# Two transformer blocks in one launch: TensorE's instructions keep the task list's order

## The chip, the cores and the metric

The kernel runs on one core of a Trainium2 chip. A core has a matrix engine (TensorE, PE in the profile), three engines for everything else (VectorE or DVE, ScalarE or ACT, GpSimd or POOL) and DMA queues that are fed by SyncE (SP). Each engine works through its own list of instructions in order, and the engines wait for each other by semaphores. The metric is the device time of one execution in microseconds.

## The reference

A sequence of 256 tokens of width 1024 goes through two blocks, all in float32. The first has two layers; the second mixes a linear recurrence with attention and ends in a gated MLP. Cut to what matters here:

```python
# first block, layer l (pooling mixer for l = 0, local attention for l = 1)
proj = rmsnorm(h, norm_mix[l]) @ w_in[l]
main, mq = proj[..., :768], proj[..., 768:]
main_out = pool_mixer(main, pool_w[l], pool_scale[l])        # l = 0: window sums, then 4 groups of 192 x 192
main_out = swa_sink_attention(q, k_shared, v_shared, sinks)  # l = 1: 12 heads of 64, window 128
mem_out = memory_attention(rmsnorm(mq), mk, mv)              # 4 heads of 64, 256 memory positions
h = h + concat([main_out, mem_out]) @ w_out[l]
h = h + relu(rmsnorm(h) @ w_up[l]) ** 2 @ w_down[l]          # width 4096

# second block
hq, hf, hi, hg, aq, ak, av, gl = split(rmsnorm(x) @ w_in)    # 8 heads of 128 each, gates of 2 x 1024
y_hg = hgrn2_mix(hq, hf, hi, hg, ...) @ w_branch_hg          # recurrence; its output times silu(hg)
y_at = moba_attention(rmsnorm(aq), rmsnorm(ak), av, rel) @ w_branch_attn   # one block of 256: causal
x = x + (sigmoid(gl[0]) * y_hg + sigmoid(gl[1]) * y_at) @ w_out
x = x + (silu(h2 @ w_gate) * (h2 @ w_up)) @ w_down           # h2 = rmsnorm(x)
```

## The kernel before

**Products.** A large product x @ w is split into rounded high and low parts and summed as xh·wh + xl·wh + xh·wl (L152, `mm`), in a rounded float32 type. Weights come by DMA into `raw` tiles; ScalarE casts the high half `wh` (L245), VectorE subtracts for the low half `wl` (L246). The activations get `xh` and `xl` in the same way. Scores, attention values, the pooling product and transposes (L159, `tr`) stay in plain float32; in the trace such a matmul has two records.

**Banks.** TensorE writes only to PSUM, of which there are eight banks of 512 float32 columns per partition: four with the tag `acc` and four with the tag `mm`, taken in turn. Instructions that share a bank are ordered by the framework: a matmul that writes into a bank which VectorE or ScalarE has yet to read, as the program has it, waits for that read, also where other columns of the bank are meant.

**What sets the order.** The parts of the work (a projection, one half of the tokens in an attention, an MLP) are Python generators, added to a list by `line.add(rank, task)`. `line.run` asks, at each step, the task of lowest rank whose time has come for its next piece. Time is `line.now`, which only `mm` and `tr` advance (by columns at the full clock); a task gives its own guess of how long its results take by `yield 6.0` and the like. This is the task list's order. After it, the framework's scheduler orders the instructions of each engine anew, by its own model of when each could start. Only in the start, inside `with tc.manual_schedule(engines={ET.DVE, ET.Activation, ET.Pool, ET.PE})` (L727), does it leave all four engines in the order written.

**The places that the change touches.**

- `pool_mix` (layer 0). For three banks in turn, two column pieces k each: the products with `pw` and `u` (L152), then ScalarE takes the high half out of the bank (L941, `xh<-mm,cols`) and VectorE the low half (L942, `xl<-mm,cols,xh`). The even and the odd piece of a bank are of one bank. Some pieces consist of two products of 128 rows, others of four of 64 rows.
- `mem_attention`. Two halves of the tokens (tt), four heads: four score products into two `acc` banks, alternating between them (and between the upper and lower 64 rows), maxima (L884), exponentials (L889), reciprocals (L891), scaling, transposes, values.
- `swa` (layer 1). `score(i)` gives two heads a bank each; VectorE reads each with bias and minimum in one instruction (L1036).
- `attend` (second block). `score(hp)` puts two heads into one bank, one behind the other. For each, VectorE adds the position bias, takes the minimum and writes to SBUF (L1411, with the accumulator's read as a second instruction), ScalarE exponentiates (L1413):

```python
for i in range(2):
    mm(ps[:, i, :nk], aq[tt][:, hd, :], ak[hd // 4][:, hd % 4, :nk])
    V.tensor_tensor_reduce(sc[:, i, :nk], ps[:, i, :nk], rel..., nm[:, c])
    A.activation(sc[:, i, :nk], sc[:, i, :nk], AF.Exp, ..., accum_out=sm[:, c])
V.reciprocal(sm[:, c2], sm[:, c2])
```

- `sides` runs beside `attend` in the list: weight products of the recurrence's gate, whose sigmoid (L1480) needs another function table on ScalarE than the exponential, and the two multiplications L1481 and L1482 on VectorE.

Of the kernel before, what the change touches and what calls it, by code (L numbers as in the profile page):

```python
# [41 lines left out]
def kernel(  # L42
# [8 lines left out]
    nc = tc.nc  # L51
    V, A, G, PE = nc.vector, nc.scalar, nc.gpsimd, nc.tensor

    const = ctx.enter_context(tc.tile_pool(name="const", bufs=1))
    wpool = ctx.enter_context(tc.tile_pool(name="wpool", bufs=1))
    keep = ctx.enter_context(tc.tile_pool(name="keep", bufs=1))
# [94 lines left out]
    def mm(out_, lhsT, rhs, start=True, stop=True):  # L151
        PE.matmul(out_, lhsT, rhs, start=start, stop=stop)  # L152
        n = math.prod(rhs.shape[1:])
        m = math.prod(lhsT.shape[1:])
        side_by_side = 4 if m <= 32 else 2 if m <= 64 else 1
        line.now += max(n, min(m, 64)) / 2400.0 * (1 if rhs.dtype == F32R else 4) / side_by_side + 0.0025
# [5 lines left out]
    def acc_bank():  # L162
        return psum.tile([P, 512], F32, tag="acc", name="acc", bufs=4)

    def mm_bank():
        return psum.tile([P, 512], F32, tag="mm", name="mm", bufs=4)
# [7 lines left out]
    def tok(tt):  # L174
        return slice(tt * P, (tt + 1) * P)
# [51 lines left out]
    def load_units(segs, nk, row0, g, apart=0):  # L227
        for k0 in range(0, nk, KU):
            raw = wpool.tile([P, KU, 512], F32, tag="raw", name="raw", bufs=5)
            c = 0  # L230
            for w, c0, cw in segs:
                r = w[row0 + k0 * P: row0 + (k0 + KU) * P, c0:c0 + cw].rearrange("(k p) c -> p k c", p=P)
                for k in range(KU if k0 < apart else 1):
                    ks = slice(k, k + 1) if k0 < apart else slice(0, KU)
                    nc.sync.dma_start(raw[:, ks, c:c + cw], r[:, ks, :])  # L235
                c += cw
            wh = wpool.tile([P, KU, 512], F32R, tag="wh", name="wh", bufs=8)
            wl = wpool.tile([P, KU, 512], F32R, tag="wl", name="wl", bufs=8)

            tc.cur_priority += 30  # L240
            if g is None:
                n = 1 if k0 < apart else KU
                for k in range(0, KU, n):
                    ks = slice(k, k + n)
                    A.copy(wh[:, ks, :], raw[:, ks, :])  # L245
                    V.tensor_sub(wl[:, ks, :], raw[:, ks, :], wh[:, ks, :].bitcast(F32))  # L246
            else:
                for k in range(KU):
                    gk = gcols[:, g + k0 + k:g + k0 + k + 1]
                    A.activation(wh[:, k, :], raw[:, k, :], AF.Copy, scale=gk)  # L250
                    V.scalar_tensor_tensor(wl[:, k, :], raw[:, k, :], gk, wh[:, k, :].bitcast(F32),  # L251
                                           op0=ALU.mult, op1=ALU.subtract)
            tc.cur_priority -= 30
            yield [(wh[:, k, :], wl[:, k, :]) for k in range(KU)]
# [61 lines left out]
    def lin(acc, xt, w, start=True, stop=True):  # L316

        n = len(w)
        for k in range(n):
            (xh, xl), (wh, wl) = xt[k], w[k]  # L320
            mm(acc, xh, wh, start and k == 0, False)
            mm(acc, xh, wl, False, False)
            mm(acc, xl, wh, False, stop and k == n - 1)
            if k % 2:
                yield 0
# [29 lines left out]
    def ktiles(t, tt=None):  # L355
        ts = slice(0, S) if tt is None else tok(tt)
        return [(t[0][:, k, ts], t[1][:, k, ts]) for k in range(t[0].shape[1])]
# [347 lines left out]
    def raw_T():  # L705

        return [act.tile([P, KT // 2, S], F32, tag="raw_T", name="raw_T", bufs=4) for _ in range(2)]

    def load_T(t, src, k, n):
        nc.sync.dma_start(t[k // 4][:, k % 4:k % 4 + n, :],  # L710
                          src[k * P:(k + n) * P, :].rearrange("(k p) t -> p k t", p=P))
# [11 lines left out]
        V.tensor_sub(xs[1][:, o, :], r, xs[0][:, o, :].bitcast(F32))  # L723

    pw = act.tile([P, 6, 192], F32, tag="pw", name="pw")
    ET = mybir.EngineType
    with tc.manual_schedule(engines={ET.DVE, ET.Activation, ET.Pool, ET.PE}):  # L727

        x_raw, m_raw = raw_T(), raw_T()

        warm = mm_bank()
        for _ in range(12):
            PE.matmul(warm[:, :P], ones, ones, start=True, stop=True)

        def units_of(i, **a):
            key, w = plan[i][:2]
            ready[key] = []
            units = load_units(*w, **a)

            def more():  # L740
                ready[key] += next(units)
                return ready[key][-KU:], len(ready[key]) - KU

            return more

        def columns_T(ps, xs, w, k, c0):

            for i, (wh, wl) in enumerate(w):
                xh, xl = ktiles(xs)[k + i]
                c = slice(c0, c0 + P)  # L750
                for j, (a, b) in enumerate(((wh, xh), (wh, xl), (wl, xh))):
                    mm(ps, a[:, c], b, k + i + j == 0, k + i == KT - 1 and j == 2)

        def rows(accs, xs, w, k):
            for tt in range(TT):
                run(lin(accs[tt], ktiles(xs, tt)[k:k + KU], w, k == 0, k + KU == KT))

        load_T(x_raw, xT, 0, 2)
        ups = [acc_bank()[:, :S] for _ in range(4)]
        more = units_of(0, apart=1)  # L760
        for k in range(0, KT, KU):
            if k:
                load_T(x_raw, xT, k, 2)
            split_raw(x_raw, xs0, k, 2, G_MIX)
            w, _ = more()
            for i in range(4):
                columns_T(ups[i], xs0, w, k, i * P)
        ups += [mm_bank()[:, :S] for _ in range(2)]
        more = units_of(1)
        pool_short()  # L770
        ws = []
        for k in range(0, KT, KU):
            w, _ = more()
            ws += w
            for i in range(2):
                columns_T(ups[4 + i], xs0, w, k, i * P)
        for tt in range(TT):
            nc.sync.dma_start(h[tt], x[0, tok(tt), :])
        nc.sync.dma_start(cols, columns)
        for k in range(0, KT, 4):  # L780
            load_T(m_raw, memT, k, 4)

        dg = act.tile([P, TT, P], F32, tag="dg", name="dg")
        nx = [Norm(h[tt]) for tt in range(TT)]
        for tt in range(TT):
            for c in range(2):
                nx[tt].add(c)
            x_r[tt] = nx[tt].rstd()
            V.tensor_scalar(dg[:, tt, :], ident, x_r[tt], None, op0=ALU.mult)
        split_raw(m_raw, mem_set, 0, 4)  # L790
        qs = mm_bank().rearrange("p (t c) -> p t c", t=TT)
        rb = act.tile([P, S], F32, tag="rb", name="rb")
        more = units_of(2)

        def queries(tt):
            run(lin(qs[:, tt, :], ktiles(xs0, tt), [(wh[:, 256:], wl[:, 256:]) for wh, wl in ws]))

        queries(0)
        ps = mm_bank()[:, :S]
        for tt in range(TT):  # L800
            PE.matmul(ps[:, tok(tt)], ones, dg[:, tt, :], start=True, stop=True)
        A.copy(rb, ps)
        queries(1)
        for i in range(2):
            V.tensor_tensor(u[:, i, :], ups[i], rb, ALU.mult)
        w, k = more()
        accs1 = [acc_bank() for _ in range(2)]
        rows(accs1, mem_set, w, k)
        split_raw(m_raw, mem_set, 4, 4)
        for i in range(2, 4):  # L810
            V.tensor_tensor(u[:, i, :], ups[i], rb, ALU.mult)
        rows(accs1, mem_set, *more())
        for i in range(4, 6):
            V.tensor_tensor(u[:, i, :], ups[i], rb, ALU.mult)
        for tt in range(TT):
            A.activation(mq[tt], qs[:, tt, :], AF.Copy, scale=x_r[tt])
        m = [act.tile([P, D], F32, tag="raw_T", name="mem", bufs=4) for _ in range(TT)]
        tc.keep_in_program_order(nc.sync.dma_start(m[0], mem[0, tok(0), :]))
        rows(accs1, mem_set, *more())
        tc.keep_in_program_order(nc.sync.dma_start(m[1], mem[0, tok(1), :]))  # L820
        mem_r[0] = row_norm(m[0])
        rows(accs1, mem_set, *more())
        mem_r[1] = row_norm(m[1])
        nc.gpsimd.dma_start(pw, pool_w[0].rearrange("g a d -> (g a) d").rearrange("(j p) d -> p j d", p=P))
        for e in mem_there:
            e.at()
# [761 lines left out]
```

## Time and profile before

| | |
|---|---|
| median of 3 runs | 1039.11 us (1039.04 to 1039.41) |
| the profiled execution | 1038.09 us, of which 1036.1 us from its first to its last instruction (the span) |
| TensorE busy | 1025.5 us (99%) |
| VectorE, ScalarE, GpSimd busy | 639.7 (62%), 562.8 (54%), 99.1 us (10%) |
| DMA | 186.40 MB, 180 GB/s on average |
| mean granted TensorE clock | 0.999 of full speed |
| chain that ended last | TensorE 96%, VectorE 1%, GpSimd 1%, DMA 1% |

Busy time of TensorE includes time in which a matmul is in the array while the next could not yet start at its best, so 99% does not say that the array is at its peak. The chain that ended last goes back from the last instruction to what released it, step by step; 96% on TensorE means that nearly everywhere the next matmul waited only for the one ahead of it.

### The profile page before, as it was taken

The numbers are of one execution on the slowest core, as the hardware profiler recorded it, in microseconds if no ns is written. First come the engines' busy times: TensorE is split into PE (matmuls) and PEld (weight loads), VectorE is DVE, ScalarE is ACT, GpSimd is POOL, SyncE is SP. The second block draws the span as 40 slices with busy tenths as digits, with TensorE's granted clock in tenths as the row PEclk, the third lists the DMA queues.
The fourth block names the chain that finished last, engine by engine and source line by source line (L and its number), as shares of the span: only waits on it lengthen the run. The fifth ranks groups of instructions, "written<-read, shape, count | busy, mean of one in ns | idle before, by whom it ended". The sixth has DMA issues, their size and how long they took to land.

```text
span 1036.1 us, 18404 instructions
## 1 busy us (share of the span) xinstructions
PE 1025.5 (99%) x7352; PEld 904.8 (87%) x7352; DVE 639.7 (62%) x1001; ACT 562.8 (54%) x901; POOL 99.1 (10%) x143
## 2 busy tenths in 40 slices
PE   8999999999999999999999999999999999999998
PEld 8768989998876788899988988888999988999997
DVE  5886655556668666464576569847635766464552
ACT  6775554454678654454465444758644555344351
POOL 1515000000143000000000004330000000000000
PEclk9999999999999999999999999999999999999999
DMA  9754556546642258656557544344365566565741
GB/s 320 269 181 136 181 184 211 191 163 204 202 164 82 57 189 317 210 185 213 173 182 235 193 165 153 119 137 145 119 203 180 169 196 210 164 211 164 234 144 41
DMA packets 107749, 186.40 MB, mean 180 GB/s; under 512 B 6792, under 2 KB 31632, under 8 KB 107664
## 3 DMA queue, kind: packets, MB, share of 16 engines
q1 hardware_dynamic: 106560, 180.43, 53.4%
q0 software_dynamic: 1104, 4.80, 1.4%
q8 instruction: 57, 0.93, 0.4%
q14 instruction: 28, 0.23, 0.1%
HBM read 182.58 MB, written 2.63 MB: 179 GB/s over the span
## 4 chain that ended last, share of the span: by engine, by line
PE 96%; DVE 1%; POOL 1%; DMA 1%; ACT 0%; issue 0%; SPq 0%; ACTq 0%
PE acc L152 59%; PE mm L152 33%; PE mm L159 3%; DMA raw<-in_w_in_dram 1%; POOL win L921 0%; DVE wl L251 0%; DVE wl L246 0%; POOL st L419 0%; POOL win L920 0%; POOL st L348 0%; ACT wh L250 0%; DVE win L921 0%; ACT wh L245 0%; ACT xh L722 0%; SPq L235 0%
## 5 line engine op out<-in xcount | busy, mean ns | idle before, releaser
L246 DVE TENSOR_TENSOR wl<-raw,wh 128x1024 fp32r<-128x1024 f32 (+1 forms) x315 | 378.1, 1223 | 172.2 <-ACT wh L245 165.6
L245 ACT CAST wh<-raw 128x1024 fp32r<-128x1024 f32 (+1 forms) x315 | 322.3, 1047 | 170.7 <-PE acc L152 101.8
L152 PE MATMUL mm<-xh,wh 128*128 128x256 f32 x752 | 208.4, 277 | 0.0
L152 PE MATMUL mm<-xl,wh 128*128 128x256 f32 x752 | 208.0, 277 | 0.0
L152 PE MATMUL mm<-xh,wl 128*128 128x256 f32 x752 | 207.9, 277 | 0.0
L152 PEld LDWEIGHTS mm<-xh,wh 128*128 128x128 f32 x752 | 141.2, 188 | 1.4 <-issue 0.4
L152 PEld LDWEIGHTS mm<-xl,wh 128*128 128x128 f32 x752 | 141.3, 188 | 1.0
L152 PEld LDWEIGHTS mm<-xh,wl 128*128 128x128 f32 x752 | 141.3, 188 | 0.0
L152 PE MATMUL acc<-wh,xh 128*128 128x512 f32 x336 | 138.3, 412 | 1.2 <-ACT wh L250 1.2
L152 PE MATMUL acc<-wh,yl 128*128 128x512 f32 x342 | 134.8, 394 | 0.0
L152 PE MATMUL acc<-wl,yh 128*128 128x512 f32 x342 | 134.0, 392 | 0.0
L152 PE MATMUL acc<-wl,xh 128*128 128x512 f32 x336 | 132.4, 394 | 1.1 <-DVE wl L251 1.1
L152 PE MATMUL acc<-wh,yh 128*128 128x512 f32 x342 | 133.4, 390 | 0.0
L152 PE MATMUL acc<-wh,xl 128*128 128x512 f32 x336 | 132.6, 395 | 0.0
L152 PE MATMUL acc<-xh,wh 128*128 128x256 f32 x416 | 117.1, 281 | 1.0 <-ACT wh L245 1.0
L152 PE MATMUL acc<-xh,wl 128*128 128x256 f32 x416 | 116.5, 280 | 1.2 <-DVE wl L246 1.2
L152 PE MATMUL acc<-xl,wh 128*128 128x256 f32 x416 | 116.2, 279 | 0.0
L152 PEld LDWEIGHTS acc<-xh,wl 128*128 128x128 f32 x416 | 78.7, 189 | 1.8 <-DVE wl L246 1.8
L152 PEld LDWEIGHTS acc<-xh,wh 128*128 128x128 f32 x416 | 78.6, 189 | 1.6 <-ACT wh L245 1.6
L152 PEld LDWEIGHTS acc<-xl,wh 128*128 128x128 f32 x416 | 78.2, 188 | 0.0
L152 PEld LDWEIGHTS acc<-wh,xh 128*128 128x128 f32 x336 | 63.2, 188 | 16.0 <-issue 2.5
L152 PEld LDWEIGHTS acc<-wl,yh 128*128 128x128 f32 x342 | 64.2, 188 | 13.7
(240 smaller groups left out, 1277.6 us busy)
## 6 DMA issues: line engine op xcount, KB each, us to landing
raw<-in_w_in_dram SPq DMA_DIRECT2D x87, 512.0 KB, 4.7
raw<-in_w_up_dram SPq DMA_DIRECT2D x64, 512.0 KB, 4.8
raw<-in_w_down_dram SPq DMA_DIRECT2D x64, 512.0 KB, 4.8
raw<-in_w_out_dram SPq DMA_DIRECT2D x24, 512.0 KB, 4.6
raw<-in_w_ffn_gate_dram SPq DMA_DIRECT2D x44, 256.0 KB, 4.3
raw<-in_w_ffn_up_dram SPq DMA_DIRECT2D x44, 256.0 KB, 4.6
raw<-in_w_ffn_down_dram SPq DMA_DIRECT2D x22, 512.0 KB, 5.3
raw<-in_w_mem_kv_dram SPq DMA_DIRECT2D x8, 512.0 KB, 9.4
```

The source lines that it names most:

```text
L152: PE.matmul(out_, lhsT, rhs, start=start, stop=stop)
L159: PE.transpose(out_, in_, ident)
L245: A.copy(wh[:, ks, :], raw[:, ks, :])
L246: V.tensor_sub(wl[:, ks, :], raw[:, ks, :], wh[:, ks, :].bitcast(F32))
```

## The change

The whole kernel is put under `manual_schedule` for TensorE, and TensorE leaves the inner one:

```diff
+    ET = mybir.EngineType
+
+    ctx.enter_context(tc.manual_schedule(engines={ET.PE}))
     const = ctx.enter_context(tc.tile_pool(name="const", bufs=1))
...
     pw = act.tile([P, 6, 192], F32, tag="pw", name="pw")
-    ET = mybir.EngineType
-    with tc.manual_schedule(engines={ET.DVE, ET.Activation, ET.Pool, ET.PE}):
+    with tc.manual_schedule(engines={ET.DVE, ET.Activation, ET.Pool}):
```

TensorE's instructions then stand in the order in which the task list gives them. The scheduler still orders the other engines outside the start. Line numbers after the change are higher by 3 up to L723 and by 2 from there on (L152 is then L155, L942 is L944, L1411 is L1413), numbers in the names by 2. On the DMA queue SP nothing moves; VectorE and ScalarE change little. TensorE's order differs in three places.

First place, TensorE in the layer-0 mixer. `mm_733` is the first bank of the pooling product (`mm_735` after the change), `mm_768` and `mm_777` the second and third (`mm_770`, `mm_779`); `acc_718` is a weight product, `acc_746` and `acc_747` are memory scores. Before:

```order
L152 MATMUL mm_733<-u_94,pw_98 128x256 [waits DMASW0_49,PE_49]
L152 MATMUL mm_733<-u_94,pw_98 128x256
L152 MATMUL mm_768<-u_94,pw_98 128x256 [waits DVE_49,Activation_49]
L152 MATMUL mm_768<-u_94,pw_98 128x256 [waits DVE_49]
L152 MATMUL acc_718<-wh_546,xh_88 128x512
L152 MATMUL mm_777<-u_94,pw_98 64x256 [waits DVE_49,Activation_49]
L152 MATMUL acc_746<-mkT0_568,mqT_593 128x256 [waits Activation_49]
```

The same place after the change:

```order
L155 MATMUL mm_735<-u_96,pw_100 128x256 [waits DMASW0_49,PE_49]
L155 MATMUL mm_735<-u_96,pw_100 128x256
L155 MATMUL mm_735<-u_96,pw_100 64x256 [waits DVE_49]
L155 MATMUL mm_735<-u_96,pw_100 64x256 x3
L155 MATMUL acc_748<-mkT0_570,mqT_595 128x256 [waits Activation_49]
L155 MATMUL acc_749<-mkT0_570,mqT_595 128x256
L155 MATMUL acc_748<-mkT0_570,mqT_595 128x256
L155 MATMUL acc_749<-mkT0_570,mqT_595 128x256
L155 MATMUL mm_770<-u_96,pw_100 128x256 [waits PE_49]
L155 MATMUL mm_770<-u_96,pw_100 128x256
L155 MATMUL mm_770<-u_96,pw_100 128x256 [waits DVE_49]
```

The second piece of the first bank (64x256) stands directly behind the first piece; before, it comes eighteen rows later. The wait on DVE is for the low half (L944) of the first piece.

Second place, TensorE in the local attention of layer 1: `acc_3229` and `acc_3233` are the scores of two heads of one group (`acc_3231` and `acc_3235` after). Before, the second one stood behind six weight products and two transposes. After the change:

```order
L155 MATMUL acc_3231<-skT_2810,qT_3169 128x256 [waits DVE_49]
L155 MATMUL acc_3235<-skT_2810,qT_3169 128x256 [waits DVE_49]
L155 MATMUL acc_3138<-wh_2918,xh_1112 128x512
L155 MATMUL acc_3138<-wl_2919,xh_1112 128x512
L155 MATMUL acc_3138<-wh_2918,xl_1113 128x512
```

The second score now stands ahead of the weight products, with its own wait on VectorE.

Third place, TensorE in the attention of the second block: `acc_7481` is the bank of two heads of the first token half, `acc_7494` that of the second half (`acc_7483` and `acc_7496` after); `acc_7435` is the gate's weight product. Before:

```order
L152 MATMUL acc_7481<-ak_5528,aq_5526 128x128 [waits Activation_49]
L152 MATMUL acc_7494<-ak_5528,aq_5527 128x256 [waits Activation_49]
L152 MATMUL acc_7435<-wh_7380,xh_3770 128x512
L152 MATMUL acc_7481<-ak_5528,aq_5526 128x128 [waits DVE_49]
L152 MATMUL acc_7435<-wl_7381,xh_3770 128x512
L152 MATMUL acc_7494<-ak_5528,aq_5527 128x256 [waits DVE_49]
L152 MATMUL acc_7435<-wh_7380,xl_3771 128x512
```

The third head pair of each token half after the change (`acc_7551`, `acc_7569`; `mm_7545` and `mm_7561` are transposes of the first pair):

```order
L162 MATMUL mm_7545<-ident_76,sc_7482 128x128 x2
L155 MATMUL acc_7551<-ak_5531,aq_5528 128x128
L155 MATMUL acc_7551<-ak_5531,aq_5528 128x128 [waits DVE_49]
L162 MATMUL mm_7561<-ident_76,sc_7495 128x128 x4
L155 MATMUL acc_7569<-ak_5531,aq_5529 128x256
L155 MATMUL acc_7569<-ak_5531,aq_5529 128x256 [waits DVE_49]
```

In each of the eight pairs the two heads now stand directly one behind the other, and the second waits for VectorE's read of the first.

## Rows read from the trace of the kernel before

**Rows 1.** The page: span, and each engine's busy time, share and instructions

```profile
span 1036.1 us, 18404 instructions
...
PE 1025.5 (99%) x7352; PEld 904.8 (87%) x7352; DVE 639.7 (62%) x1001; ACT 562.8 (54%) x901; POOL 99.1 (10%) x143
```

**Rows 2.** Waits of TensorE, largest and last of seven: us in total, times, longest

```profile
PE acc L152 <- ACT wh L250: 1.2, 1, 1.2
...
PE mm L152 <- issue: 0.5, 1, 0.5
```

**Rows 3.** Timeline, TensorE, place 1: start us, us, engine, line, operation, idle before

```profile
53.43 1.86 PE L152 MATMUL mm<-u,pw 128*128 128x256 f32 x8
54.94 0.58 PE L152 MATMUL acc<-wh,xh 128*128 128x512 f32 x1
...
56.08 1.13 PE L152 MATMUL acc<-mkT,mqT 64*128 64x256 f32 x8
...
58.70 1.22 PE L152 MATMUL mm<-u,pw 64*64 64x256 f32 x4 [0.92 <-DVE u L926]
59.85 1.13 PE L152 MATMUL acc<-mkT,mqT 64*128 64x256 f32 x4
60.91 0.51 PE L152 MATMUL acc<-wl,xh 128*128 128x512 f32 x1
61.25 0.40 PE L152 MATMUL acc<-wh,xl 128*128 128x512 f32 x1
61.48 0.40 PE L152 MATMUL acc<-wh,xh 128*128 128x512 f32 x1
...
62.73 1.80 PE L152 MATMUL mm<-u,pw 128*64 128x256 f32 x8
...
80.94 0.39 PE L152 MATMUL acc<-wh,xh 128*128 128x512 f32 x1
```

**Rows 4.** Timeline, VectorE, place 1

```profile
55.52 1.21 DVE L246 TENSOR_TENSOR wl<-raw,wh 128x1024 fp32r<-128x1024 f32 x1
...
60.15 1.22 DVE L246 TENSOR_TENSOR wl<-raw,wh 128x1024 fp32r<-128x1024 f32 x1
...
61.35 0.48 DVE L942 SCALAR_TENSOR_TENSOR xl<-mm,cols,xh 128x256 fp32r<-128x256 f32 x1
```

**Rows 5.** Windows at the end: length, busy PE, PEld, DVE, ACT, POOL, PEclk, DMA

```profile
1034.00:1035.00 1.00, 0.00 (x0) 0.00 (x0) 0.00 (x0) 0.00 (x0) 0.00 (x0) 0.93 0.33 111
1035.00:1036.10 1.10, 0.00 (x0) 0.00 (x0) 0.00 (x0) 0.00 (x0) 0.00 (x0) 0.50 0.00 0
```

**Rows 6.** Windows at the start, warm-up line: length, busy PE, PEld, PEclk, DMA

```profile
2.00:3.00 1.00, 1.00 (x7) 1.00 (x6) 1.00 0.53 85
...
4.00:5.00 1.00, 1.00 (x10) 1.00 (x10) 1.00 1.05 303
```

**Rows 7.** Timeline, TensorE, place 2

```profile
313.29 0.70 PE L152 MATMUL acc<-skT,qT 64*128 64x256 f32 x2
```

**Rows 8.** Timeline, VectorE, place 2

```profile
314.52 0.47 DVE L1036 CUSTOM_DVE_ANT_0 sc<-acc,bias,nsink 128x256 f32<-128x256 f32 x1
```

**Rows 9.** Timeline, TensorE, place 3

```profile
705.19 0.82 PE L152 MATMUL acc<-ak,aq 128*128 128x128 f32 x4
705.65 0.58 PE L152 MATMUL acc<-wh,xh 128*128 128x512 f32 x1
706.07 0.47 PE L152 MATMUL acc<-ak,aq 128*128 128x128 f32 x2
...
706.64 0.70 PE L152 MATMUL acc<-ak,aq 128*128 128x256 f32 x2
```

**Rows 10.** Timeline, VectorE, place 3

```profile
705.71 0.29 DVE L1411 CUSTOM_DVE_ANT_0 sc<-acc,rel 128x128 f32<-128x128 f32 x1 [1.64 <-PE acc L152]
...
707.38 0.42 DVE L1411 CUSTOM_DVE_ANT_0 sc<-acc,rel 128x256 f32<-128x256 f32 x1 [0.49 <-PE acc L152]
```

**Rows 11.** Timeline, ScalarE, place 3

```profile
710.61 1.28 ACT L1480 ACT_TABLE_LOAD   x1
```

## The prediction

> **What bounds the kernel now.** I read the page's busy line first, then the list of TensorE's waits, then the timelines of TensorE, VectorE and ScalarE around the places where the two orders differ. TensorE is busy 1025.5 of 1036.1 us [rows 1]; in its list of waits seven entries add up to 7.0 us, the largest 1.2 us, the last 0.5 us [rows 2]. So a different order can win back little idle time, and any new wait comes straight out of the end: no later stretch has TensorE idle, so no later stretch can absorb it. What the scheduler's order does cost today is hidden in busy time. A matmul issued behind one of the other kind (plain float32 against the rounded type of the weight products) has about 0.33 us instead of 0.23 us to the next (60.91 to 61.25, then 61.48) [rows 3]; and the first score pair of the memory attention, issued bank by bank, takes 1.13 us for two matmuls (59.85), as long as four of them take where the two row halves alternate (56.08) [rows 3]; the trace counts each twice.
>
> **What the change moves.** Adding no operation and taking none away, it leaves TensorE with the task list's order. That list counts time only by TensorE's own work and by fixed guesses, and knows nothing of a PSUM bank that VectorE must read before TensorE may write it again. The orders differ in three places.
>
> **Place 1, the pooling product of the first layer.** Before, eighteen rows of other work stand between the two column pieces of the first bank. Now the second stands directly behind the first, and waits for VectorE's L942 (the low half of the first piece), because both pieces share a bank. VectorE does that at 61.35, 0.48 us long, behind four weight splits of 1.22 us, the first from 55.52, the last from 60.15 [rows 4]; its queue up to there is unchanged. The first piece runs from 53.43, two matmuls of 0.38 us (four take 1.51 us until 54.94) [rows 3], and about 0.2 us later now, because one weight product that covered a wait ahead of it has gone. So TensorE stops at 54.4 and goes on at 61.35 + 0.48 + 0.07 = 61.90: a wait of 7.5 us. Replaying the rest on the same durations: second piece 1.73 us (four products, 1.80 us busy before [rows 3], the next issued 0.07 sooner) to 63.6, scores 1.06 to 64.7, third piece 0.76 to 65.45, a wait of 1.4 (its low half follows two maxima and a ScalarE copy), pieces four and five to 69.35, a wait of 1.15 (the low half follows the softmax scaling), the sixth, the turns and scores of the second half to 73.35, twelve weight products to 76.2, a wait of 1.2 for the turned weights, and so on: the first product of the output projection's next group, at 80.94 before [rows 3], comes at about 87.5. That is 11.25 us of waits, of which 6.6 us remain: 0.92 us of idle before goes [rows 3], 1.06 us through the scores, some 2.7 us through twelve fewer changes of kind (10 instead of 22 in this stretch) and a piece of work that stood between. I take **+6.6**, ends 5 and 8.
>
> **The clock in that wait.** [...] Behind the wait stands 3.55 us of plain float32 work. Nothing lost is one end, twice as long (+3.5) the other. Nearest is the kernel's start, where 7 warm-up matmuls fall in the third microsecond and 10 in the fifth [rows 6], although the clock column reads 1.00 throughout: three microseconds at seven tenths lose 0.9. I take **+1.0**.
> [...]
>
> **Place 2, the local and memory attention of the second layer.** The second score of a head pair now follows the first directly, and waits for VectorE's read of another score out of its bank: the read at L1036 starts at 314.52 and takes 0.47 us, 1.2 us behind the score that it reads, issued at 313.29 [rows 7, 8]. That wait is about 1.4 us in place of three weight products. Six further waits of 0.15 to 1.05 us follow behind copies on ScalarE (the turned weights, behind exponentials and weight casts): 4.4 us in all. The replay gives 2.6 us of it back, what this stretch loses today to changes of kind and hidden waits, and ends 1.8 us later. I take **+1.8**, ends 0.5 and 3.5.
>
> **Place 3, the scores of the second block.** Two heads share a bank; the second product must wait until VectorE has read the first (L1411). Before, a weight product lies between. With VectorE free, the price of a pair can be read: product at 705.19, read from 705.71 to 706.00, second product at 706.07 [rows 9, 10]. That is 0.88 us instead of 0.23: 0.65 us idle. For 128x256 the read starts 0.74 us behind the product (706.64 to 707.38) and takes 0.42 us [rows 9, 10]; with the same 0.07 us to TensorE that is 1.23 us instead of some 0.35: 0.9 us idle. Four pairs of each: 6.2 us. Against it, each of eight inserted weight products no longer costs 0.42 instead of 0.23 us (705.65 to 706.07): 1.6 us back. So 4.6 us at least.
> On top, VectorE is not free at three pairs, since its queue is in order and its scheduler put a gate and reciprocals ahead of the reads. The gate needs a table load of 1.28 us on ScalarE [rows 11], a sigmoid, and another load before the next exponential. By the replay the read of the first product of the third head pair (acc_7551, first token half) comes at 715.3 instead of right behind 714.0: idle 1.65 us, 1.0 over the plain price. Its neighbour (acc_7569, second token half) waits behind a weight split that waits for a cast, and a reciprocal: 2.75 us, 1.85 over. The fourth pair (acc_7653) waits behind the second gate, itself behind a table load: 3.2 us, 2.55 over. With 0.5 us of smaller delays: 4.6 + 5.4 + 0.5 = **+10.5**, ends 4.6 and 14. The other engines gain nothing that TensorE could use, and SP's queue of loads is not moved.
>
> **Sum.** The profiled execution took 1038.09 us, 2.0 more than its span, 1.0 less than the median 1039.11. 1038.1 + 6.6 + 1.0 + 1.8 + 10.5 = 1058.0 for such an execution, 1059 as a median.
>
> **Rivals.**
> *Only the floor.* VectorE's late reads turn out early, because what it waits for on ScalarE was late only through TensorE's own order: place 1 +5, no clock loss, place 2 +0.5, place 3 +4.6: 1038.1 + 10.1 + 1.0 = 1049. For it: my replay carries delays on, and errors there add up. Against: the order of VectorE's and ScalarE's queues is known, and their durations are.
> *The clock falls more often.* The waits of 2.75 and 3.2 us in place 3 and the shorter ones of place 1 each lose about 1 us more: 1062 to 1064. For it: at the end, too, the clock fell within microseconds of the last matmul. Against: TensorE works right up to these waits.
> *Faster.* The changes of kind and the score order, which with the idle cost 4.6 + 2.6 + 1.6 = 8.8 us today, go away, and the waits do not come: above all, if VectorE reads the first pooling piece ahead of its four weight splits, the wait at place 1 shrinks by 4 x 1.22 us from 7.5 to 2.6 us, and that place ends under 2 us worse. It decides in favour of the new order when all waits together stay under 8.8 us; with half of them it would end near 1035. Against: four weight splits stand ahead of that read in VectorE's queue in both orders, and they are as long as measured.
> *The order hardly matters*, since the waits listed are met by the time TensorE gets there: 1039. Against: the wait on L942 alone has a date, 61.83.
>
> **How the numbers follow.** Forecast 0.62, own range 1052 to 1065; only the floor 0.20; clock more often 0.12; faster 0.03; hardly matters 0.03. The range that holds 8 in 10 reaches from the floor's 1049 to 1066. A measurement of this kernel tells about 0.2%, 2.1 us, from no change: faster 0.03, same 0.03, slower 0.94.
>
> **What would show it.** Right: TensorE idle for 7 us or more from about 54.4, released by L944 (the low half); eight waits on L1413 between 705 and 740 in the changed kernel's time, three of them over 1.5 us; TensorE's list of waits grown from 7 to about 30 us, and 12 fewer changes of kind around 60 us. Wrong: VectorE's low half well ahead of 61 us; score waits all under 1 us; a granted clock below 1.00 behind the short waits; or a later stretch shorter than before, which I hold impossible.

## The result, and the profile after

The changed kernel takes 1065.26 us (median of 4 runs, 1064.83 to 1068.27), the kernel before 1039.22: a ratio of 1.0256, 95% interval 1.0239 to 1.0274. It is 26 us slower; 1059 was forecast, with a range of 1049 to 1066.

The profiled execution is the slowest of the four, 1068.27 us with a span of 1066.1; the other spans are 1062.7 to 1063.5. The page of the changed kernel, busy time and share of each engine, and the shares of the chain that ended last (compare [rows 1]):

```profile
PE 1037.3 (97%) x7352; PEld 911.5 (85%) x7352; DVE 640.6 (60%) x1001; ACT 564.0 (53%) x901; POOL 100.8 (9%) x143
...
PE 93%; DVE 3%; ACT 2%; POOL 1%; issue 1%; DMA 1%; SPq 0%; DVEq 0%; ACTq 0%
```

The number of instructions is the same, and VectorE and ScalarE are as busy as before. TensorE is busy 11.8 us more for the same work: that is not waiting. What it waits for, in us in total, times, longest (compare [rows 2]):

```profile
PE acc L155 <- DVE s L1413: 8.9, 8, 3.5
PE mm L155 <- DVE xl L944: 7.8, 3, 5.6
PE acc L155 <- DVE s L1038: 1.4, 2, 1.1
PE mm L155 <- issue: 1.3, 1, 1.3
```

All entries together make 25.2 us instead of 7.0. So the span's 30.0 us are 18.2 us of waits and 11.8 us of slower work. The slower work is the clock: cut into windows, with each window's busy time multiplied by its granted clock, TensorE's work comes to 1025 us in this trace, as in the one before, and 12.3 us of busy time are lost to a granted clock below 1.00. The windows around place 1 show it. The columns are the window's length, busy time (and count) of PE, PEld, DVE, ACT and POOL, the granted clock, the DMA share and GB/s:

```profile
54.00:58.00 4.00, 2.20 (x11) 1.29 (x9) 3.94 (x11) 3.55 (x7) 1.92 (x1) 0.99 0.21 48
58.00:62.00 4.00, 0.15 (x1) 0.15 (x2) 3.94 (x8) 0.00 (x0) 0.51 (x1) 0.87 0.78 253
62.00:66.00 4.00, 4.00 (x12) 1.56 (x14) 1.32 (x2) 0.47 (x1) 1.32 (x2) 0.50 0.97 322
66.00:70.00 4.00, 2.92 (x12) 1.60 (x8) 2.05 (x6) 1.43 (x5) 0.00 (x0) 0.78 0.19 73
70.00:74.00 4.00, 3.82 (x12) 1.07 (x10) 1.96 (x7) 1.74 (x8) 0.00 (x0) 0.65 0.00 0
74.00:78.00 4.00, 3.10 (x9) 2.16 (x10) 0.66 (x2) 0.81 (x2) 0.00 (x0) 0.50 0.02 4
78.00:82.00 4.00, 4.00 (x18) 2.76 (x17) 1.71 (x5) 0.86 (x2) 0.00 (x0) 0.57 0.00 0
```

The clock falls in the long wait, to 0.50 from 61 us on, and is back at full speed only near 81 us, with a short recovery near 68 us (1.00 from 68 to 71). TensorE and VectorE there (timeline: start us, us, engine, line, operation, idle before and its releaser; compare [rows 3, 4]):

```profile
54.98 1.22 PE L155 MATMUL mm<-u,pw 128*128 128x256 f32 x4
61.85 3.21 PE L155 MATMUL mm<-u,pw 128*64 128x256 f32 x8 [5.65 <-DVE xl L944]
64.99 2.08 PE L155 MATMUL acc<-mkT,mqT 64*128 64x256 f32 x8
...
69.62 4.21 PE L155 MATMUL mm<-u,pw 128*128 128x256 f32 x12 [1.08 <-DVE xl L944]
74.91 2.37 PE L155 MATMUL mm<-u,pw 64*128 64x256 f32 x4 [1.08 <-DVE xl L944]
```

```profile
60.11 1.22 DVE L249 TENSOR_TENSOR wl<-raw,wh 128x1024 fp32r<-128x1024 f32 x1
...
61.31 0.48 DVE L944 SCALAR_TENSOR_TENSOR xl<-mm,cols,xh 128x256 fp32r<-128x256 f32 x1
```

The second pooling piece is issued at 61.85; 61.90 was worked out. But it takes 3.21 us busy, where 1.80 stood before, and the four scores 2.08 instead of 1.13. (In this one execution the clock was also low, at 0.50, from about 50.8 to 54, ahead of the pooling product, which began 1.55 us later than before. The scheduler's order was no protection from that in `p3_block2` below, which leaves this stretch to the scheduler: its mean clock from 50 to 54 us is 0.61. The other three executions, 3 us shorter, are the ones to compare with.)

Place 3, TensorE, with each pair's second product and its wait (compare [rows 9]):

```profile
723.17 0.38 PE L155 MATMUL acc<-ak,aq 128*128 128x128 f32 x2
724.04 0.92 PE L155 MATMUL acc<-ak,aq 128*128 128x128 f32 x4 [0.49 <-DVE s L1413]
725.60 0.70 PE L155 MATMUL acc<-ak,aq 128*128 128x256 f32 x2 [0.64 <-DVE s L1413]
...
731.89 0.39 PE L155 MATMUL acc<-ak,aq 128*128 128x128 f32 x2
733.47 0.49 PE L155 MATMUL acc<-ak,aq 128*128 128x128 f32 x2 [1.19 <-DVE s L1413]
...
734.23 0.60 PE L155 MATMUL acc<-ak,aq 128*128 128x256 f32 x2
736.40 0.70 PE L155 MATMUL acc<-ak,aq 128*128 128x256 f32 x2 [1.57 <-DVE s L1413]
...
745.85 0.39 PE L155 MATMUL acc<-ak,aq 128*128 128x128 f32 x2
749.78 0.49 PE L155 MATMUL acc<-ak,aq 128*128 128x128 f32 x2 [3.55 <-DVE s L1413]
```

The plain pair follows itself after 0.87 us (723.17 to 724.04; 0.88 was read from the kernel before). The longest wait is the one behind the second gate: on ScalarE a table load of 1.28 us starts at 745.87 and VectorE's two gate products stand ahead of the read ([rows 11] shows such a load before).

How late the work is at marks that are the same matmuls in both traces: at 83.69 us of before (the transposes behind the first mixer) 14.0 us late, at the first score of place 3 (705.19 before, 723.17 now) 18.0, at the value products behind the last pair (729.95 before, 760.00 now) 30.05. From there to the end nothing is lost or won.

### The profile page after: what moved, and what is told of

It reads as the page before. It is cut to its first block, busy times and chain, and to the rows that moved or that the text cites. A ratio compares the mean times of both kernels' runs of the same rounds, so it can differ in the third digit from the quotient of the medians.

```text
span 1066.1 us, 18415 instructions
## 1 busy us (share of the span) xinstructions
PE 1037.3 (97%) x7352; PEld 911.5 (85%) x7352; DVE 640.6 (60%) x1001; ACT 564.0 (53%) x901; POOL 100.8 (9%) x143
## 4 chain that ended last, share of the span: by engine, by line
PE 93%; DVE 3%; ACT 2%; POOL 1%; issue 1%; DMA 1%; SPq 0%; DVEq 0%; ACTq 0%
PE acc L155 57%; PE mm L155 33%; PE mm L162 3%; DVE wl L249 1%; DMA raw<-in_w_in_dram 1%; POOL win L923 0%; DVE wl L254 0%; ACT sc L1040 0%; ACT wh L248 0%; DVE sc L1413 0%; DVE win L923 0%; ACT eT L451 0%; DVE u L928 0%; POOL st L422 0%; POOL win L922 0%
## 5 line engine op out<-in xcount | busy, mean ns | idle before, releaser
L155 PE MATMUL mm<-xh,wh 128*128 128x256 f32 x752 | 208.2, 277 | 0.0
L155 PE MATMUL mm<-xl,wh 128*128 128x256 f32 x752 | 207.8, 276 | 0.0
L155 PE MATMUL mm<-xh,wl 128*128 128x256 f32 x752 | 207.7, 276 | 0.0
L155 PEld LDWEIGHTS mm<-xh,wh 128*128 128x128 f32 x752 | 141.2, 188 | 1.4 <-issue 0.4
L155 PEld LDWEIGHTS mm<-xl,wh 128*128 128x128 f32 x752 | 141.3, 188 | 1.0
L155 PEld LDWEIGHTS mm<-xh,wl 128*128 128x128 f32 x752 | 141.2, 188 | 0.0
L155 PE MATMUL acc<-wh,xh 128*128 128x512 f32 x336 | 138.4, 412 | 1.2 <-ACT wh L253 1.2
L155 PE MATMUL acc<-wh,yl 128*128 128x512 f32 x342 | 134.7, 394 | 0.0
L155 PE MATMUL acc<-wl,yh 128*128 128x512 f32 x342 | 134.0, 392 | 0.0
L155 PE MATMUL acc<-wl,xh 128*128 128x512 f32 x336 | 132.5, 394 | 0.9 <-DVE wl L254 0.9
L155 PE MATMUL acc<-wh,yh 128*128 128x512 f32 x342 | 133.4, 390 | 0.0
L155 PE MATMUL acc<-wh,xl 128*128 128x512 f32 x336 | 132.7, 395 | 0.0
L155 PE MATMUL acc<-xh,wh 128*128 128x256 f32 x416 | 117.0, 281 | 0.7 <-ACT wh L248 0.7
L155 PE MATMUL acc<-xh,wl 128*128 128x256 f32 x416 | 116.3, 280 | 1.0 <-DVE wl L249 1.0
L155 PE MATMUL acc<-xl,wh 128*128 128x256 f32 x416 | 116.1, 279 | 0.0
L155 PEld LDWEIGHTS acc<-xh,wl 128*128 128x128 f32 x416 | 78.7, 189 | 1.4 <-DVE wl L249 1.4
L155 PEld LDWEIGHTS acc<-xh,wh 128*128 128x128 f32 x416 | 78.7, 189 | 1.2 <-ACT wh L248 1.1
L155 PEld LDWEIGHTS acc<-xl,wh 128*128 128x128 f32 x416 | 78.1, 188 | 0.0
L155 PEld LDWEIGHTS acc<-wh,xh 128*128 128x128 f32 x336 | 63.6, 189 | 15.6 <-issue 1.8
L155 PEld LDWEIGHTS acc<-wl,yh 128*128 128x128 f32 x342 | 64.2, 188 | 13.7
```

## The experiments

**One place at a time.** The inner `manual_schedule` for TensorE is entered ahead of one stage and left behind it; the rest is as before:

```diff
+    pe_order = tc.manual_schedule(engines={ET.PE})
+    pe_order.__enter__()
...
     line.run(...)          # the stage of the place
+    pe_order.__exit__(None, None, None)
```

> TensorE keeps the list's order only up to the end of the first layer's mixer (place 1), the scheduler orders the rest. Theory: the loss sits in three places and adds up; place 1 alone gives 12 to 14 us of it (in the trace of the changed kernel the work after this place is 14.0 us late, of which 1.6 us was lost ahead of the pooling product): 1051 to 1053. Rival: the loss is spread over the kernel, by TensorE's order everywhere: this one loses less than half of place 1's share, under 1046.

> TensorE keeps the list's order only in the second layer's mixer (place 2). Theory: 4.0 us by the trace of the changed kernel, about 1.8 of them by the low clock: 1043. Rival: the waits there are a consequence of the delay brought in from place 1 (weights and buffers late): no loss, 1039.

> TensorE keeps the list's order only in the second block's mixer (place 3). Theory: 12.1 us by the trace of the changed kernel, eight waits on the score read of together 8.9 us: 1051. Rival: without the delays brought in from the other places the reads are in time, and only the plain price of the pairs is left, 4.6 us: 1044.

Measured beside 1038.75 us for the kernel before: place 1 1047.73 (ratio 1.0089, 1.0074 to 1.0104), place 2 1041.97 (1.0033, 1.0021 to 1.0045), place 3 1053.83 (1.0146, 1.0129 to 1.0163). That is +9.0, +3.2 and +15.1, together 27.3 us, about the loss of the whole change: it sits in these three places and adds up. Place 1 came out under its 12 to 14, place 2 under its 4.0 and place 3 over its 12. Place 1 was read from the slowest execution of the changed kernel. Here the same waits cost less, since the clock, low from about 58.5 to 65.5 (means of 0.56 from 58 to 62 us and 0.59 from 62 to 66), came back and stayed up behind both waits of 1.08 us (1.00 in every window from 66 to 86 us):

```profile
61.72 3.21 PE L156 MATMUL mm<-u,pw 128*64 128x256 f32 x8 [6.92 <-DVE xl L945]
...
68.33 3.06 PE L156 MATMUL mm<-u,pw 128*128 128x256 f32 x12 [1.08 <-DVE xl L945]
```

```profile
66.00:72.00 6.00, 4.31 (x18) 1.65 (x16) 3.98 (x13) 3.50 (x11) 0.00 (x0) 1.00 0.12 47
```

From the first pooling piece to the transposes behind the first mixer the low clock costs 1.8 us in this trace and 7.5 in the changed kernel's (busy time of each window, times what its granted clock lacks to 1.00). The six executions of place 2 differ in the same way: the three with a mean clock of 0.999 or 1.000 took 1040.36 to 1041.62 us, the three with 0.996 or 0.997 took 1042.32 to 1043.62. Place 3 says most, since its waits are the same as in the changed kernel, 8.9 us:

```profile
PE acc L152 <- DVE s L1413: 8.9, 8, 3.5
```

From the first score to the value products this run needs 41.0 us (706.50 to 747.51), the changed kernel 36.8 (723.17 to 760.00), the kernel before 24.8 (705.19 to 729.95). The 4.2 us between the two with the same waits are the clock, which costs 5.9 us in this trace and 1.5 in the changed kernel's. Windows of this run, and of the changed kernel:

```profile
720.00:725.00 5.00, 5.00 (x16) 3.96 (x16) 1.72 (x7) 2.10 (x6) 0.00 (x0) 0.67 0.36 105
...
735.00:740.00 5.00, 4.47 (x17) 3.70 (x17) 1.29 (x7) 1.84 (x7) 0.00 (x0) 0.50 0.00 0
740.00:745.00 5.00, 5.00 (x16) 3.94 (x15) 1.22 (x5) 0.67 (x4) 0.00 (x0) 0.62 0.00 0
```

```profile
750.00:755.00 5.00, 4.47 (x21) 3.62 (x21) 1.60 (x8) 1.94 (x7) 0.00 (x0) 0.66 0.00 0
755.00:760.00 5.00, 5.00 (x23) 4.08 (x22) 2.22 (x7) 2.71 (x4) 0.00 (x0) 1.00 0.00 0
```

Run by itself, place 3 had the clock low behind two waits, of 1.56 and 3.55 us; in the changed kernel only behind the longest, of 3.55 us.

**A bank for each reader.** The changed kernel, with `acc_bank()` inside the loop over the two heads of `attend` and `mm_bank()` inside the loop over the pieces of `pool_mix`:

```diff
-            ps = acc_bank().rearrange("p (h k) -> p h k", k=S)
             for i in range(2):
+                ps = acc_bank().rearrange("p (h k) -> p h k", k=S)
```

> The changed kernel, but every head's score in the second block and every column piece of the pooling product takes a PSUM bank of its own (the four banks of a tag then come round twice as fast). Theory: TensorE waits because two pieces share a bank; the second piece at place 1 no longer waits for the first's low half, only the fourth bank later does, and the first pairs at place 3 don't wait: a loss of 8 to 16 us instead of 26, 1047 to 1055. Rival: the readers are late whatever the bank, and with the banks coming round faster the same waits stand one piece later: 1062 to 1068.

Measured: 1046.42 (1.0081, 1.0066 to 1.0096), just better than the 1047 to 1055 of the theory and far from the rival's 1062. The waits on the score read are gone from the list, and the clock stays at 1.00 through place 3:

```profile
PE mm L162 <- DVE me L455: 2.0, 1, 2.0
...
PE acc L155 <- DVE hgate L1483: 1.0, 2, 0.7
...
PE mm L155 <- DVE xl L944: 0.8, 1, 0.8
```

At the mark behind the first mixer it is 2.8 us late (86.45 against 83.69), and place 3 takes 26.7 us (710.77 to 737.49), 2.0 more than before. The same stretch of this run, and of the kernel before (window, busy time, clock):

```profile
710.77:737.49 26.72, 25.68 (x129) 20.60 (x128) 18.73 (x66) 21.34 (x48) 0.00 (x0) 1.00 0.34 113
```

```profile
705.19:729.95 24.76, 24.76 (x130) 20.77 (x128) 18.73 (x66) 21.45 (x48) 0.00 (x0) 1.00 0.35 119
```

So sharing a bank with a slow reader is the cause of most of the loss at places 1 and 3. The list's order itself wins nothing at place 3: without the bank waits and at the full clock TensorE is still busy 0.9 us longer there than before.

**Holding the clock, or shortening the wait.** The first run puts 32 matmuls of ones between the first two pooling pieces; the second moves the split of the pooling product ahead in ScalarE's and VectorE's queues:

```diff
+                if k == 0:
+                    spare = acc_bank()
+                    for _ in range(32):
+                        PE.matmul(spare[:, :P], ones, ones, start=True, stop=True)
                 xh, xl = (t[:, k, :] for t in xs)
```

```diff
+                tc.cur_priority -= 3000
                 A.activation(xh, ps[:, k - k0, :], AF.Copy, scale=col(V_PSCALE + k))
                 V.scalar_tensor_tensor(xl, ...)
+                tc.cur_priority += 3000
```

> The changed kernel with 32 matmuls of ones (128x128 float32, into a spare bank that nobody reads) between the first and the second pooling piece, where TensorE waits some 7 us: it works there and waits no less. Theory: part of the loss is the clock, which falls in that wait and again behind the 1.1 us waits that follow; with the clock held at place 1 the kernel gets 2 to 5 us faster than the changed one, 1060 to 1063, and the granted clock reads 1.00 from 54 to 66. Rival: the clock costs nothing that the waits don't hide, and what is lost at place 1 is waiting alone: 1065, or slower by the matmuls' own overrun.

> The changed kernel with ScalarE's and VectorE's split of the pooling product moved ahead in their queues by a higher priority: one weight split stands ahead of the first low half instead of four. Theory: the 7 us wait at place 1 is VectorE's queue; it shrinks to under 4 us (the second piece then waits for the last pooling sums on VectorE until about 57), and 3 to 6 us of the loss go: 1059 to 1062. Rival: the wait ends with something else that is late anyway (the pooling sums of the second piece, the weights): under 2 us are won, 1063 to 1065.

Measured: 1066.01 (1.0259, 1.0243 to 1.0276) and 1066.67 (1.0259, 1.0236 to 1.0281): neither wins anything, and the theory's numbers were missed twice. The traces say why. With the wait filled, the clock is at 1.00 until 68 us, and then falls behind the next, 1.1 us long wait, as it does in the windows below; the long wait itself, now work of no use, is still there.

```profile
67.00:68.00 1.00, 0.75 (x3) 0.42 (x4) 0.36 (x2) 1.00 (x5) 0.00 (x0) 1.00 0.04 14
68.00:69.00 1.00, 1.00 (x4) 0.46 (x4) 0.72 (x3) 1.00 (x5) 0.00 (x0) 0.73 0.00 0
69.00:70.00 1.00, 1.00 (x4) 0.29 (x4) 0.96 (x4) 0.23 (x1) 0.00 (x0) 0.50 0.00 0
```

With the low half moved ahead, the wait is 2.22 us, and the second piece starts at 57.69 instead of 61.85. But the clock still falls, at 59 us, and stays low until 76 us (three of the windows):

```profile
57.69 1.80 PE L155 MATMUL mm<-u,pw 128*64 128x256 f32 x8 [2.22 <-DVE xl L945]
59.42 2.08 PE L155 MATMUL acc<-mkT,mqT 64*128 64x256 f32 x8
```

```profile
59.00:60.00 1.00, 1.00 (x4) 0.54 (x5) 0.94 (x3) 0.47 (x1) 0.00 (x0) 0.69 0.97 377
...
66.00:68.00 2.00, 2.00 (x6) 0.59 (x8) 1.48 (x2) 1.01 (x3) 1.47 (x1) 0.50 0.21 82
...
76.00:77.00 1.00, 1.00 (x7) 0.48 (x6) 0.27 (x1) 0.00 (x0) 0.00 (x0) 0.78 0.00 0
```

At the mark it is 10.2 us late, with the fillers 9.3, and with neither cure 9.0 (in the run of place 1 by itself; the 14.0 of the changed kernel are from its slowest execution). Against that run, the earlier low half saves 4.7 us of waiting and pays 5.7 us more to the clock (7.5 instead of 1.8). The fillers keep the wait as work, and the clock costs 1.6 us one wait later. The theory that came out of this: each cure alone is paid back, by the clock or by the wait.

**Both cures together**, on the kernel that has only place 1 in the list's order (1047.73). The diffs are the two above, with 14, 6 and 6 matmuls of ones behind the first, third and fifth piece.

> Place 1 alone in the list's order (the run that took 1047.7), with both cures together: the low halves go ahead of the weight splits in VectorE's queue, and what is left of the three waits is filled with matmuls of ones (14, 6 and 6 of them, into a spare bank that nobody reads). Theory: taken alone the cures win nothing because a shorter wait is paid back by the clock, and a held clock leaves the long wait; together they win 4 to 6 us, 1042 to 1044, with the granted clock at 1.00 from 54 to 76. Rival: the loss at place 1 is neither wait nor clock but the work that TensorE does in a worse order (nothing is left to put beside the pooling product): 1047 to 1049 again.

Measured: 1043.69 (1.0048, 1.0033 to 1.0063), 4 us better than place 1 alone, and the intervals don't meet. The granted clock is 1.00 in every window from 50 to 86 us, and TensorE is 5.0 us late at the mark (88.66) instead of 9.0 (92.67):

```profile
54.95 3.39 PE L946 MATMUL acc<-ones 128*128 128x128 f32 x28
58.27 1.80 PE L156 MATMUL mm<-u,pw 128*64 128x256 f32 x8
60.00 1.13 PE L156 MATMUL acc<-mkT,mqT 64*128 64x256 f32 x8
```

The same scores take 1.13 us again, and not 1.33 as in the run of place 1 alone, or 2.08. Of the gain, 1.8 us are the clock and 2.3 the shorter waits (9.7 us of idle time there, 7.3 of idle time and fillers here). So at place 1 both are shown: the wait on VectorE's queue, and the clock behind it.

**Telling the list of the readers.** The changed kernel, where the list's own clock is made to pass between the pieces of a bank, so that other work is put there; the second run does so in the second layer too.

```diff
-            yield 6.0 if k0 == 0 else 0
...
             for k in (k0, k0 + 1):
+                yield (6.0, 7.4, 0, 2.4, 0, 2.4)[k]
...
+                if i:
+                    yield 1.2          # attend, between two heads of a bank
...
+                if j:
+                    yield 0.8          # swa, between two heads (second run only)
```

> The changed kernel, with TensorE in the list's order, but the list is told of the shared banks: between the two pieces of a pooling bank the task waits 7.4 (2.4) us of the list's time, between the two heads of a score pair 1.2 us, so that it puts weight products there. Theory: the loss was the order's ignorance of the readers and nothing else; places 1 and 3 cost nothing any more, place 2 is as in the changed kernel: 1039 to 1044. Rival: a fixed order can't follow the real times of the other engines, and the scheduler's fine interleaving is worth more: over 1048.

> As the run before, and in the second layer's local attention the list waits 0.8 us between two heads' scores as well. Theory: the 3 us of place 2 go as well, and fewer changes between float32 and the weight products' type win something over the kernel before: 1034 to 1040. Rival: place 2's waits are those on ScalarE's copies and exponentials, which this doesn't change: as the run before, 1041 to 1044.

Measured: 1053.98 (1.0147, 1.0129 to 1.0166) and 1066.34 (1.0262, 1.0203 to 1.0321). The first is 11 us better than the changed kernel and 10 worse than the theory allowed; it lies where the rival had it, over 1048. The list put the scores of the second token half into the gap, and these take a bank whose last contents ScalarE and VectorE have not yet read, because VectorE is still in its weight splits:

```profile
PE acc L155 <- ACT me L891: 6.8, 1, 6.8
```

The wait at place 1 had only changed its bank: at the first score of the second layer the run is 8.8 us late (313.21 against 304.39), nearly as much as with place 1 alone. The second run missed what the theory and the rival gave; it has two kinds of executions, 1060.7 to 1060.9 and 1071.8 to 1072.3, with a mean clock of 0.992 to 0.994 and 0.980 to 0.981. In the profiled one of the latter kind some 20 us are lost in the second layer, 13.7 of them to the clock. Behind a wait of 2.2 us, TensorE is busy without a gap in this layer's attention and still runs at a clock of 0.50:

```profile
330.00:340.00 10.00, 10.00 (x40) 5.73 (x40) 4.51 (x20) 6.32 (x18) 1.83 (x4) 0.50 0.01 2
340.00:350.00 10.00, 10.00 (x45) 7.15 (x43) 8.47 (x31) 6.76 (x21) 2.53 (x3) 0.50 0.18 52
```

**Is there something to win in the kernel before?** Its scheduler with a bank for each reader, and its scheduler with only the four score products of a token half kept together.

```diff
+        with tc.manual_schedule(engines={ET.PE}):
             for hp in range(2):
                 for i in range(2):
                     rows = slice(i * 64, i * 64 + 64)
```

> The kernel before, with its scheduler, and a bank for every head's score in the second block and every pooling piece. Theory: under the scheduler TensorE has nearly no wait left, so the banks win at most the 0.9 us at the pooling sums and some changes of kind: 1036 to 1039. Rival: with the banks coming round twice as fast the scheduler has less freedom: 1039 to 1043.

> The kernel before, with only the four score products of each token half of the memory attention kept in the written order, which alternates between the 64-row halves of the array. Theory: the one pair of halves that the scheduler pulls apart bank by bank (1.13 us for two products, as long as four) is put together, 0.5 to 1.1 us: 1037.9 to 1038.4, at the edge of what can be told. Rival: keeping the four together makes one of them wait, 1039 or slower.

Measured: 1038.10 (0.9998, 0.9990 to 1.0007) and 1038.36 (1.0006, 0.9995 to 1.0017). No difference can be told. In the second run the products kept their order, but other work still came between the first of the second half (59.71) and the other three (67.22), so its question, what a split pair costs, stays open. No version here beats the kernel before.

## Why the prediction was right, and which term was mis-sized

The direction, the three places and the mechanism were right: what TensorE may not overtake any more is a reader of its own bank, which stands behind other work in its own engine's queue (at place 1 the low half at 61.31 us, behind the weight split at 60.11). The forecast was 6 us short: the result lies at the upper edge of the range of 1049 to 1066 and just outside the forecast's own 1052 to 1065. Added up by the terms, the waits less what comes back were right to 1 or 2 us, and the clock is the rest:

| us | waits | less what comes back | clock |
|---|---|---|---|
| prediction | 27.8 | 8.8 | 1.0 |
| the three runs of one place each | 20.1 more than before | 0.8 | 7.7 |
| changed kernel, slowest execution | 18.2 more than before | 0.5 | 12.3, of which 1.7 ahead of place 1 |

The measured rows are worked out from windows of the traces: idle time; busy time times the granted clock, against the kernel before; and busy time times what the clock lacks to 1.00. (0.9 us of idle time that goes at place 1 is in the prediction's 8.8, and is already taken off the measured waits.)

*The wait at place 1* was to end at 61.90 and ended at 61.85. It was put at 7.5 us and is 5.65 in the changed kernel, where TensorE came 1.55 us late, and 6.92 in the run of place 1 alone. The two later ones were put at 1.4 and 1.15 us and read 1.08 each, and the wait for the turned weights, put at 1.2, is 0.18 there and 0.6 in the run of place 1 alone. In that run the place cost 9.0 us. With both cures, when the clock stayed up, it cost 5.0. The forecast was 7.6.

*The clock in that wait* is the term that was mis-sized: "I take +1.0", from nothing lost to +3.5, for one fall at place 1 alone. The +3.5 is the author's estimate from the 0.50 that [rows 5] show at the kernel's end, the +1.0 one from the pace of its start ([rows 6], with the clock column at 1.00); no run shows a fall behind a wait that costs 1.0. Measured in its place: 7.7 us in the runs of one place each (1.8 at place 1, none at place 2, 5.9 at place 3), and 10.7 at the three places of the changed kernel's slowest execution (7.5, 1.7 and 1.5). At place 1 alone the term was nearly right; at places 2 and 3 it was put at nothing. It was thought to be one stretch of 3 us behind one wait. The runs showed it low for some 17 us behind a wait of 2.2 us (0.50 from 60 to 76 us), and in some traces again behind waits of 1.1 us (0.50 from 72 to 81 us in the changed kernel's), with short float32 products and more waits as the work that follows. In the run of place 1 alone the clock stayed up behind the same two waits of 1.08 us. In the second of the runs that tell the list of the readers it stayed at 0.50 for 20 us without any further wait (330 to 350 us). So further waits were not needed for that; what decides in which execution it falls, and for how long, stays open. The prediction's own sign of being wrong, "a granted clock below 1.00 behind the short waits", came true. The rival *the clock falls more often* (1062 to 1064) came nearer to 1065 than the forecast, and it was held too unlikely at 0.12.

*Place 2* was put at 1.8, as 4.4 us of waits less 2.6, and cost 3.2 alone and 4.0 in the changed kernel. There the clock falls too, near 330 us (0.50 from 331 to 334); in the profiled run of the place alone it stays up, and that execution (1040.36, a span of 1038.2) is 2.1 us over before. In its trace the waits of the place are 2.4 us and 0.5 come back, so that it costs 1.9: near the 1.8, by two sizes that were both 2 us too high.

*Place 3* was put at 10.5: 12.1 in the changed kernel, 15.1 alone. The waits were right in kind and order: the product after the third pair's first 1.58 us later (1.65 + 0.23 worked out), the fourth pair's 3.93 (3.2 + 0.23), the one between them 2.17 instead of 3.1. What was missing is the clock behind the longest ones. TensorE's list of waits grew to 25.2 us where about 30 was the sign, and two of the waits on the score read are over 1.5 us where three were. *Only the floor* (4.6 us there) fell with these rows; *faster* and *hardly matters* with the result.

*What the change gives back*, changes of kind and short hidden waits, was taken as 8.8 us. Twelve changes of kind fewer were counted, and the traces have twelve fewer at place 1 (8 instead of 20); but at the 0.1 us each of [rows 3] they make 1.2 us, not the greater part of 2.7. At place 1 the work at the full clock falls from 29.3 to 27.6 us and 0.9 us of idle time goes, so that 2.6 us come back, where 4.6 was put in. At place 2 it is 0.5 instead of 2.6, and at place 3, where 1.6 was put in, TensorE's work is longer by 1.4 us. The waits were put too high by nearly as much, in part because the profile ends a wait's idle time where the prediction did not: a product ahead of a wait is busy for 0.38 us, and for 0.23 to the next one without a wait. That the two errors cancel is luck. Filling the waits of places 2 and 3 was not tried.

## What to carry to other kernels

An order of instructions that is fixed by one engine's own time has to know who reads the bank that it writes next: ask, for each matmul, which engine must have read its bank, and what stands in that engine's queue ahead of the read. Where a scheduler is switched off, give such pieces banks of their own first; here that took back some 19 of 26 us. And price a wait of TensorE by what follows it, too: behind a wait of 2.2 us the same products took nearly twice as long for up to 17 us (four scores 2.08 us instead of 1.13), while in another run they were as fast as before behind waits of 1.1 us (1.14 us). So one trace of a kernel does not settle what its waits cost.

## What the runs showed of the hardware that had not been expected

The granted clock did not come back with the end of a wait. In the run with the low half moved ahead it was low from 59 to 76 us, behind 2.2 us without work (0.69 in the first of these windows, then 0.50), though TensorE was busy for 14.8 of these 17 us, and in one execution of the second run that tells the list of the readers it stayed at 0.50 for 20 us in which TensorE had no gap at all (330 to 350 us, small float32 products and transposes). Shortening the wait from 5.6 to 2.2 us left the time unchanged (1065.26 and 1066.67), since the clock fell to 0.50 in both.

The clock was not the same from one execution to the next. The two waits of 1.08 us at place 1 left it at 1.00 in one trace (66 to 86 us) and had it at 0.50 behind them in another (72 to 81 us). The same eight waits cost 12.1 us in one kernel and 16.2 in another (41.0 less 24.8), and the two kinds of executions of one program lie 11 us apart.
